# Eight strips of a Strassen-multiplied up-projection opened ahead of the norm, their partial sums kept in DRAM

## The chip, the cores and the metric

One Trainium2 chip, one core. The metric is the device time of one execution in microseconds (us). The engines are named as in the profile: PE is TensorE, DVE is VectorE, ACT is ScalarE, POOL is GpSimd, SP is SyncE, whose queue issues the DMAs. Each engine works through its instructions in order.

## What is computed

A decoder trunk of two layers on 1024 tokens of width 1024, in float32. Layer 0 mixes tokens by a gated linear recurrence (HGRN2, 8 heads), layer 1 by latent attention (MLA, 8 heads). Each mixer is followed by a gated feed-forward network of width 2816 with a causal convolution of three taps, and that is what the change is about:

```python
def _conv_ffn(h, w_up, conv_w, conv_b, w_down):
    S = h.shape[1]
    u = h @ w_up
    u_pad = jnp.pad(u, ((0, 0), (FFN_CONV - 1, 0), (0, 0)))
    y = conv_b.astype(u.dtype)
    for j in range(FFN_CONV):
        y = y + u_pad[:, j:j + S, :] * conv_w[j]
    gate, up = jnp.split(y, 2, axis=-1)
    return (jax.nn.silu(gate) * up) @ w_down

def reference(...):
    ...
    for layer in range(DEPTH):
        h = _rmsnorm(x, norm_mix[layer])
        ...
        x = x + y
        h = _rmsnorm(x, norm_ffn[layer])
        x = x + _conv_ffn(h, ffn_w_up[layer], ffn_conv_w[layer], ffn_conv_b[layer], ffn_w_down[layer])
    return x
```

## The kernel before

**Layout and precision.** The residual x lies with its channels on the 128 partitions, as two tiles `xt[0]` and `xt[1]` of 8 x 512 tokens: x0 holds the first 512 tokens, x1 the last. Every float32 product is made of three matmuls: each operand is split into a high part (a cast, ACT, line 125) and a low part (a subtraction, DVE or POOL, line 128), and high x high, low x high and high x low are summed in PSUM.

**The up-projection** (`up_phase`) runs over 22 strips a layer. Strip j makes 128 gate channels and 128 up channels for all 1024 tokens. It is cut in 2 x 2 blocks (gate or up channels; lower or upper half of the input channels) against 2 x 2 blocks of the normed input (lower or upper half of the channels; x0 or x1), and multiplied in Winograd's form of Strassen's algorithm, which takes seven block products. A product (`product`, line 835) is 12 matmuls of 128 x 512. The operands on the side of the input are b11 and b21, which need x0 alone, and t1, t2, t3, r22 and t4, which need x0 and x1. On the side of the weights, `combos` (line 819) forms s1 to s4 with four adds on DVE and splits all of them; raw weights come into two `wraw` buffers of 512 KB.

The seven products of a strip are, in order: a11 b11 into a bank of PSUM named `ps_mm`, a12 b21 into `ps_wo` (the two *opening* products, which make the gate's result on the first tokens), s2 t2 on top of a11 b11 in `ps_mm`, the previous strip's last product a22 t4 (`tail`), s1 t1 on top, s3 t3 into `ps_up`, and s4 r22 on top. Between them `ps_mm` is read out by ACT copies: line 863 behind the first, 877, 881 and 886 in `middle`. DVE adds the results from `ps_wo` and `ps_up` (line 849). ACT makes the first tap of the convolution (line 842) and DVE the two others (line 845); ACT applies Silu (889), DVE multiplies gate and up (872), and the strip goes out to DRAM as `act_spill` (873), from which `down_phase` fetches it again (930). The strips' results lie where x was: `normalize` writes x to DRAM (`x_spill`, line 238) and scales it in place (line 242).

**The gap.** Ahead of strip 0 stand `first_half` (norm of x0, b11 and b21 split into the tiles hh0 and hl0) and `second_half` (norm of x1, the differences of line 261, and t2, t1, t3, r22, t4 split on DVE, line 128). `up_phase` emits the combos and the opening products of strips 0 and 1 (`start`), then `second_half`, then the rest of strip 0 and 1, and then strip by strip.

**What sets the order.** The code is written in Tile with its scheduler: the program's order gives the priorities, and a planner sets one fixed order of instructions for each engine before the run. So a block that is emitted earlier tends to stand earlier in each queue, mixed with its neighbours.

**The mixers.** In `hgrn` the loop over (head, half) units emits `first_half` when the next unit is the last (`i + 2 == len(units)`), so ahead of the last recurrence `recur`. The output matmuls `wout` (lines 144 to 146) of the last unit follow it. In `mla` each head runs `attend` for four blocks of queries; the maximum of the scores is a reduction (line 682), then a small maximum (685) and the bias of the exponential (687); the residual add is line 275. The token sums of a norm are matmuls with ones (line 164), and line 218 copies the spread scale that line 242 multiplies with.

Of the kernel before, what the change touches and what calls it, by code (L numbers as in the profile page):

```python
# [9 lines left out]
F32 = mybir.dt.float32  # L10
# [5 lines left out]
ALU = mybir.AluOpType  # L16
# [3 lines left out]
P = 128  # L20
# [38 lines left out]
def trunk_kernel(ctx: ExitStack, tc: tile.TileContext, x, pos, par, gout, cst, msk, w_hin, w_hout,  # L59
# [23 lines left out]
    acts = nc.dram_tensor("act_spill", (NFF, P, S), F32).ap()  # L83

# [150 lines left out]
    LO, HI = slice(0, KH), slice(KH, KD)  # L235

# [17 lines left out]
    def second_half(layer, ep):  # L254
# [23 lines left out]
    def hgrn(layer, h):  # L278
        with ExitStack() as st:
# [186 lines left out]
            for i, (hd, hf) in enumerate(units):  # L466
# [11 lines left out]
                if i + 2 == len(units):  # L478
                    h2 = first_half(layer)
# [27 lines left out]
    def mla(h):  # L507
        with ExitStack() as st:
# [247 lines left out]
            for hd in range(HEADS):  # L756
# [13 lines left out]
                o1 = otile()  # L770
                attend(hd, 2, kk, vv, *q1, *o1)
                wout(0, wo, o0)
# [26 lines left out]
    def up_phase(layer, h, wfp, ps_up):  # L799
        with ExitStack() as st:  # L800
# [4 lines left out]
            def combos(j):  # L805
# [7 lines left out]
                t1 = pair("w", wpool, 3)  # L813
                split(g, *t1, lo_eng=dve)
# [10 lines left out]
                def half(t, i):  # L825
                    return [x[:, i * HF:(i + 1) * HF] for x in t]

                return dict(a11=half(t1, 0), a12=half(t1, 1), s2=half(t2, 0), s4=half(t2, 1), s3=half(t3, 0),
                            s1=half(t3, 1), a22=t4)

            def product(p, a, b, first=True):
                for k in range(KH):
                    ks = slice(k * P, (k + 1) * P)
                    for n, (l, r) in enumerate(((0, 0), (0, 1), (1, 0))):
                        pe.matmul(p, lhsT=a[l][:, ks], rhs=b[:, r, k, :], start=first and k == 0 and n == 0,  # L835
                                  stop=k == KH - 1 and n == 2, skip_group_check=not first)
# [14 lines left out]
            L, R = slice(0, HF), slice(HF, S)  # L851
            ts = {}

            def start(j):
                c = combos(j)
                ug, uu = us[2 * (j % 2)], us[2 * (j % 2) + 1]
                c.update(ug=ug, uu=uu, yb=ps_mm(), wb=ps_wo())
                product(c["yb"], c["a11"], b11)
                product(c["wb"], c["a12"], b21)
                return c  # L860

            def opened(c):
                act.copy(out=c["ug"][:, L], in_=c["yb"])
                add(c["ug"][:, L], c["wb"])

            def tail(j, c):
# [8 lines left out]
            def middle(j, c, prev):  # L875
                product(c["yb"], c["s2"], t2, False)
                act.copy(out=c["uu"][:, L], in_=c["yb"])
                if prev is not None:
                    tail(j - 1, prev)
                product(c["yb"], c["s1"], t1, False)  # L880
                act.copy(out=c["uu"][:, R], in_=c["yb"])
                c["zb"] = ps_up()
                product(c["zb"], c["s3"], t3)
                add(c["uu"][:, R], c["zb"])
                product(c["yb"], c["s4"], r22, False)
                act.copy(out=c["ug"][:, R], in_=c["yb"])
                yg = ys[2 * (j % 2)]
                conv(j, c["ug"], yg)
                act.activation(out=yg, in_=yg, func=AF.Silu)
                c["yg"] = yg  # L890
# [7 lines left out]
            prev = c1  # L898
            for j in range(2, NFF):
# [131 lines left out]
```

## Time and profile before

| | before |
|---|---|
| median of 3 runs | 2642.61 us (2641.17 to 2643.84) |
| the profiled execution | 2641.39 us |
| its span in the profile | 2639.7 us |
| its mean granted TensorE clock | 0.971 |
| busy us (share): PE | 2476.8 (94%) |
| DVE | 1772.4 (67%) |
| ACT | 1048.6 (40%) |
| POOL | 503.5 (19%) |

The profile is of one execution. Times in its rows run from the start of the span. The granted clock is TensorE's, as a share of full speed (1.00 is 2.4 GHz, 0.50 is 1.2 GHz). In a row of the timeline, `[18.60 <-ACT bop L125]` says that the engine had stood idle for 18.60 us and that an ACT instruction of line 125 on tile `bop` released it. A group of several instructions is marked `x8`, and its time reaches from the first start to the last end. Layer 0's up-projection runs from about 718 us, layer 1's from about 1980 us.

### The profile page before, as it was taken

The numbers are of one execution on the slowest core, as the hardware profiler recorded it, in microseconds if no ns is written. First come the engines' busy times: TensorE is split into PE (matmuls) and PEld (weight loads), VectorE is DVE, ScalarE is ACT, GpSimd is POOL, SyncE is SP. The second block draws the span as 40 slices with busy tenths as digits, with TensorE's granted clock in tenths as the row PEclk, the third lists the DMA queues.
The fourth block names the chain that finished last, engine by engine and source line by source line (L and its number), as shares of the span: only waits on it lengthen the run. The fifth ranks groups of instructions, "written<-read, shape, count | busy, mean of one in ns | idle before, by whom it ended". The sixth has DMA issues, their size and how long they took to land.

```text
span 2639.7 us, 35284 instructions
## 1 busy us (share of the span) xinstructions
PE 2476.8 (94%) x13732; PEld 2049.1 (78%) x13732; DVE 1772.4 (67%) x3186; ACT 1048.6 (40%) x1729; POOL 503.5 (19%) x489
## 2 busy tenths in 40 slices
PE   7999999998599999999999999989839999999999
PEld 6888888886388888888887777777628888888887
DVE  7456565578767777774445888788787777775333
ACT  5222222223344444533333544444434444544322
POOL 4343333442000000000013434443300000000000
PEclk9999999998699999999999999999969999999999
DMA  3110110210122222264431000000111222226443
GB/s 143 41 41 33 38 36 24 66 57 33 56 88 72 84 84 81 94 224 152 140 116 40 9 17 17 25 17 9 41 56 71 88 74 94 74 75 221 156 170 121
DMA packets 58343, 203.03 MB, mean 77 GB/s; under 512 B 6592, under 2 KB 6976, under 8 KB 57024
## 3 DMA queue, kind: packets, MB, share of 16 engines
q1 hardware_dynamic: 58176, 200.77, 21.5%
q8 instruction: 108, 1.77, 0.3%
q14 instruction: 59, 0.48, 0.1%
HBM read 165.10 MB, written 35.65 MB: 76 GB/s over the span
## 4 chain that ended last, share of the span: by engine, by line
PE 80%; DVE 15%; ACT 2%; issue 1%; DMA 1%; POOL 0%; SPq 0%; DVEq 0%; ACTq 0%; POOLq 0%
PE ps_mm L835 19%; PE ps_up L835 9%; PE ps_up L924 7%; PE ps_mm L144 6%; PE ps_mm L146 6%; PE ps_mm L145 5%; PE ps_mm L924 4%; PE ps_wo L924 4%; PE ps_wo L835 4%; PE ps_misc L924 2%; DVE x L275 2%; PE sc L364 2%; PE ps_wo L144 2%; PE ps_wo L146 1%; PE sp L677 1%; PE ps_wo L145 1%
## 5 line engine op out<-in xcount | busy, mean ns | idle before, releaser
L125 ACT CAST whi<-wraw 128x1024 fp32r<-128x1024 f32 (+1 forms) x312 | 306.6, 991 | 619.7 <-PE ps_misc L924 234.9
L128 DVE TENSOR_TENSOR wlo<-wraw,whi 128x1024 fp32r<-128x1024 f32 (+1 forms) x266 | 298.2, 1134 | 325.6 <-ACT whi L125 325.4
L835 PE MATMUL ps_mm<-bop,whi 128*128 128x512 f32 x1408 | 446.1, 398 | 21.3 <-ACT bop L125 11.2
L835 PEld LDWEIGHTS ps_mm<-bop,whi 128*128 128x128 f32 x1408 | 268.3, 191 | 84.4 <-ACT bop L125 11.7
L845 DVE SCALAR_TENSOR_TENSOR x<-x,prm,x 128x1023 f32<-128x1023 f32 (+1 forms) x176 | 225.1, 1280 | 103.5 <-ACT x L842 102.8
L835 PE MATMUL ps_mm<-bop,wlo 128*128 128x512 f32 x704 | 277.5, 395 | 0.0
L835 PE MATMUL ps_up<-bop,whi 128*128 128x512 f32 x704 | 221.1, 395 | 36.6 <-ACT bop L125 36.6
L835 PEld LDWEIGHTS ps_up<-bop,whi 128*128 128x128 f32 x704 | 132.4, 188 | 67.6 <-ACT bop L125 37.5
L924 PE MATMUL ps_up<-ring,whi 128*128 128x512 f32 x528 | 159.3, 389 | 0.0
L835 PEld LDWEIGHTS ps_mm<-bop,wlo 128*128 128x128 f32 x704 | 134.1, 191 | 30.1
L128 POOL TENSOR_TENSOR wlo<-wraw,whi 128x1024 fp32r<-128x1024 f32 x46 | 112.3, 2444 | 221.6 <-ACT whi L125 221.3
L144 PE MATMUL ps_mm<-vgh,hh 128*128 128x256 f32 x512 | 145.1, 284 | 5.4 <-DVE q L331 5.4
L146 PE MATMUL ps_mm<-vgh,hl 128*128 128x256 f32 x512 | 145.1, 283 | 0.0
L145 PE MATMUL ps_mm<-vgl,hh 128*128 128x256 f32 x512 | 143.7, 281 | 0.0
L835 PE MATMUL ps_up<-bop,wlo 128*128 128x512 f32 x352 | 138.2, 393 | 0.0
L375 DVE TENSOR_TENSOR Q<-Q,tot 128x256 f32<-128x256 f32 x96 | 61.1, 636 | 100.8 <-PE sc L364 78.7
L677 PE MATMUL sp<-kk,qq 128*128 128x256 f32 (+4 forms) x480 | 112.2, 364 | 15.4 <-ACT pp L692 11.9
L819 DVE TENSOR_TENSOR wraw<-wraw 128x512 f32<-128x512 f32 x176 | 122.4, 695 | 1.2
L144 PE MATMUL ps_mm<-hh,whi 128*128 128x512 f32 x288 | 116.4, 404 | 2.5 <-DVE g L351 1.6
L842 ACT ACTIVATE x<-x,prm 128x1024 f32<-128x1024 f32 x88 | 109.4, 1243 | 15.3 <-DVE x L849 13.8
L377 POOL TENSOR_TENSOR K<-K,tot 128x256 f32<-128x256 f32 x96 | 77.2, 805 | 199.3 <-PE sc L364 125.4
L924 PEld LDWEIGHTS ps_up<-ring,whi 128*128 128x128 f32 x528 | 99.1, 188 | 20.5
(302 smaller groups left out, 5790.5 us busy)
## 6 DMA issues: line engine op xcount, KB each, us to landing
wraw<-in_w_up_dram SPq DMA_DIRECT2D x88, 512.0 KB, 3.8
wraw<-in_w_down_dram SPq DMA_DIRECT2D x88, 512.0 KB, 3.5
act_spill<-x SPq DMA_DIRECT2D x44, 512.0 KB, 2.6
araw<-act_spill SPq DMA_DIRECT2D x88, 256.0 KB, 3.6
wraw<-in_w_hin_dram SPq DMA_DIRECT2D x38, 512.0 KB, 3.5
x_spill<-x SPq DMA_DIRECT2D x4, 2048.0 KB, 7.3
x<-x_spill SPq DMA_DIRECT2D x4, 2048.0 KB, 8.1
wraw<-in_w_hout_dram SPq DMA_DIRECT2D x8, 512.0 KB, 3.5
```

The lines of the kernel that those rows point to most:

```text
L125: act.copy(out=hi, in_=src)
L128: lo_eng.tensor_tensor(out=lo, in0=src, in1=hi.bitcast(F32), op=ALU.subtract)
L144: pe.matmul(ps, lhsT=lh, rhs=rh, start=(i == 0), stop=False)
L145: pe.matmul(ps, lhsT=lh, rhs=rl, start=False, stop=False)
L146: pe.matmul(ps, lhsT=ll, rhs=rh, start=False, stop=(i == n - 1))
L377: pool.tensor_tensor(out=Kv[:, :, 0, :], in0=Kv[:, :, 0, :], in1=tv[:, :, 1:2].broadcast_to([P, nb, m]), op=ALU.mult)
L677: pe.matmul(sp[:, 0:n], lhsT=qq[:, a, qs], rhs=kk[:, c, cl], start=(i == 0), stop=last)
L819: dve.tensor_tensor(out=o, in0=p, in1=q, op=op)
L835: pe.matmul(p, lhsT=a[l][:, ks], rhs=b[:, r, k, :], start=first and k == 0 and n == 0, stop=k == KH - 1 and n == 2, skip_group_check=not f ...
L842: act.activation(out=y, in_=u, func=AF.Identity, scale=cw(2, ff), bias=pcol("cb", layer * 44 + ff))
L845: dve.scalar_tensor_tensor(out=y[:, i:S], in0=u[:, 0:S - i], scalar=cw(2 - i, ff), in1=y[:, i:S], op0=ALU.mult, op1=ALU.add)
L924: pe.matmul(acc[d], lhsT=w[l][:, d * P:(d + 1) * P], rhs=a[:, r], start=j == 0 and n == 0, stop=j == NFF - 1 and n == 2)
```

## The change

1. `second_half` is emitted first in `up_phase`. Behind it a new `open_strips` makes the two opening products of the eight strips 1, 3, 5, ..., 15 (`OPENED`). For each it fetches and splits the gate weights, runs a11 b11 into a `ps_mm` bank, copies it out (R), runs a12 b21 on top, and copies the sum out (L), both by ACT. The copies lie in small tiles (one buffer for R, two for L) and are stored to a DRAM tensor `open_spill`, 256 KB each.
2. In its turn, an opened strip fetches R and L from `open_spill` (512 KB) straight into the place of the gate's result, and makes five products. Its reads of `ps_mm` are then DVE adds with R, where a plain strip has ACT copies; the split of the gate weights and the add of the second opening product fall away. `start`, `opened` and `middle` become one function `strip`, and strips 0 and 1 no longer have their combos and opening products ahead of `second_half`.
3. In `hgrn`, `first_half` is emitted behind the last recurrence (`i + 1 == len(units)`), ahead of its `wout`.
4. In the last head of `mla`, the first `wout` is emitted ahead of the third `attend`.
5. t1 and t2 trade tiles with t3 and r22.

```diff
+    OPENED = tuple(range(1, 17, 2))
...
+    def open_strips(layer, h):
+        b11, b21 = h
+        for j in OPENED:
+            a11, a12 = halves(load_w(w_up[layer][j], eng=dve))
+            p = ps_mm()
+            for a, b, to, tag in ((a11, b11, R, "rb0"), (a12, b21, L, "sq")):
+                product(p, a, b, to is R)
+                t = tpool.tile([P, HF], F32, tag=tag, name="part", bufs=2 if tag == "sq" else 1)
+                act.copy(out=t, in_=p)
+                nc.sync.dma_start(out=opening[j][:, to], in_=t)
...
-        t2 = operand(f2, hpool, "hh1")
-        t1 = operand(b11, hpool, "hl1")
+        t2 = operand(f2, ep, "e0")
+        t1 = operand(b11, ep, "e1")
...
-        t3 = operand(b12, ep, "e0")
-        r22 = operand(b22, ep, "e1")
+        t3 = operand(b12, hpool, "hl1")
+        r22 = operand(b22, hpool, "hh1")
...
-                if i + 2 == len(units):
+                if i + 1 == len(units):
                     h2 = first_half(layer)
...
+                if not more:
+                    wout(0, wo, o0)
                 attend(hd, 2, kk, vv, *q1, *o1)
-                wout(0, wo, o0)
+                if more:
+                    wout(0, wo, o0)
...
-                t1 = pair("w", wpool, 3)
-                split(g, *t1, lo_eng=dve)
+                c = {}
+                if not opened:
+                    t1 = pair("w", wpool, 3)
+                    split(g, *t1, lo_eng=dve)
+                    c["a11"], c["a12"] = halves(t1)
...
+            def strip(j, prev):
+                opened = j in OPENED
+                c = combos(j, opened)
...
+                if opened:
+                    nc.sync.dma_start(out=ug, in_=opening[j])
+                else:
+                    product(yb, c["a11"], b11)
+                    act.copy(out=ug[:, L], in_=yb)
+                    wb = ps_wo()
+                    product(wb, c["a12"], b21)
+                    add(ug[:, L], wb)
+
+                def read(dst):
+                    if opened:
+                        dve.tensor_tensor(out=dst, in0=ug[:, R], in1=yb, op=ALU.add)
+                    else:
+                        act.copy(out=dst, in_=yb)
+
+                product(yb, c["s2"], t2, opened)
+                read(uu[:, L])
...
-            c0, c1 = start(0), start(1)
             t1, t2, t3, t4, r22 = second_half(layer, ep)
-            opened(c0)
-            opened(c1)
-            middle(0, c0, None)
-            middle(1, c1, c0)
...
+            open_strips(layer, h)
+            prev = None
+            for j in range(NFF):
+                prev = strip(j, prev)
+            tail(prev)
```

The planner's order shows what moves. Three places of DVE's queue follow; a row has the line, the operation, the tiles out<-in and the shape.

The first place is the end of `second_half` in layer 0. `x_73` and `x_74` are x0's and x1's tiles, `f_...` the difference of which t2 is made, `bop` an operand's low part, `wlo` that of a weight. Before:

```order
L819 TENSOR_TENSOR wraw<-wraw 128x512 x4
L128 TENSOR_TENSOR wlo<-wraw,whi 128x1024
L242 SCALAR_TENSOR_TENSOR x_74<-x_74,prm,rb 128x512 x8
L128 TENSOR_TENSOR wlo<-wraw,whi 128x1024
L261 TENSOR_TENSOR x_73<-x_74,x_73 128x2048
L128 TENSOR_TENSOR bop<-x_74,bop 128x2048
L261 TENSOR_TENSOR f_6986<-x_74,x_73 128x2048
L261 TENSOR_TENSOR x_74<-x_74 128x2048
L128 TENSOR_TENSOR bop<-x_73,bop 128x2048
L261 TENSOR_TENSOR x_73<-x_73,f_6986 128x2048
L128 TENSOR_TENSOR bop<-f_6986,bop 128x2048
L128 TENSOR_TENSOR bop<-x_74,bop 128x2048
```
And with the change:

```order
L129 TENSOR_TENSOR wlo<-wraw,whi 128x1024
L129 TENSOR_TENSOR bop<-x_73,bop 128x2048
L129 TENSOR_TENSOR wlo<-wraw,whi 128x1024
L285 TENSOR_TENSOR x_73<-x_73,f_6886 128x2048
L129 TENSOR_TENSOR bop<-f_6886,bop 128x2048
L129 TENSOR_TENSOR bop<-x_74,bop 128x2048
L129 TENSOR_TENSOR wlo<-wraw,whi 128x512
L129 TENSOR_TENSOR bop<-x_73,bop 128x2048
L870 TENSOR_TENSOR x_73<-x_73,ps_wo 128x512
L849 TENSOR_TENSOR wraw<-wraw 128x512 x4
L129 TENSOR_TENSOR wlo<-wraw,whi 128x1024 x2
L129 TENSOR_TENSOR wlo<-wraw,whi 128x512
```
The four combination adds of strip 0 (line 819, now 849), which stood ahead of x1's scaling, now stand behind the last operand, and so do the low parts made of them; low parts of the openers' weights stand between the operands.

The second place is in strips 5 and 6 of layer 0 (5 is opened), with combination adds and low parts of weights, and the adds from PSUM. Before, in such strips:

```order
L872 TENSOR_TENSOR x_74<-x_74 128x1024
L819 TENSOR_TENSOR wraw<-wraw 128x512
L128 TENSOR_TENSOR wlo<-wraw,whi 128x1024 x2
L849 TENSOR_TENSOR x_73<-x_73,ps_wo 128x512
L845 SCALAR_TENSOR_TENSOR x_74<-x_73,prm,x_74 128x1023
L845 SCALAR_TENSOR_TENSOR x_74<-x_73,prm,x_74 128x1022
L849 TENSOR_TENSOR x_73<-x_73,ps_up 128x512
L128 TENSOR_TENSOR wlo<-wraw,whi 128x1024
L128 TENSOR_TENSOR wlo<-wraw,whi 128x512
```
With the change:

```order
L849 TENSOR_TENSOR wraw<-wraw 128x512 x2
L890 TENSOR_TENSOR x_73<-x_73,ps_mm 128x512
L129 TENSOR_TENSOR wlo<-wraw,whi 128x1024
L870 TENSOR_TENSOR x_73<-x_73,ps_up 128x512
L129 TENSOR_TENSOR wlo<-wraw,whi 128x1024
L890 TENSOR_TENSOR x_73<-x_73,ps_mm 128x512
L866 SCALAR_TENSOR_TENSOR x_74<-x_73,prm,x_74 128x1023
L129 TENSOR_TENSOR wlo<-wraw,whi 128x512
L866 SCALAR_TENSOR_TENSOR x_74<-x_73,prm,x_74 128x1022
```
The new reads of `ps_mm` (line 890) stand just ahead of low parts (129), in the queue that also has the adds (870) and taps (866).

The third place is the end of the attention in layer 1, from the last low part of the probabilities (`tl`) to the bias `nb` of the last block. Before:

```order
L128 TENSOR_TENSOR tl<-ps_wo,th 128x384
L696 RECIPROCAL sm<-sm 128x1
L682 TENSOR_REDUCE mx<-sp 128x1
L819 TENSOR_TENSOR wraw<-wraw 128x512
L212 TENSOR_TENSOR acc<-acc,sq 128x512
L275 TENSOR_TENSOR x_73<-x_73,ps_mm 128x512 x2
L685 TENSOR_TENSOR mx<-mx 128x1
L819 TENSOR_TENSOR wraw<-wraw 128x512
L128 TENSOR_TENSOR ol<-ps_misc,oh 128x256
L687 SCALAR_TENSOR_TENSOR nb<-mx,rq 128x1
```
With the change:

```order
L129 TENSOR_TENSOR tl<-ps_wo,th 128x384
L706 TENSOR_REDUCE mx<-sp 128x1
L299 TENSOR_TENSOR x_73<-x_73,ps_mm 128x512
L709 TENSOR_TENSOR mx<-mx 128x1
L711 SCALAR_TENSOR_TENSOR nb<-mx,rq 128x1
L299 TENSOR_TENSOR x_73<-x_73,ps_mm 128x512
L213 TENSOR_TENSOR acc<-acc,sq 128x512
L299 TENSOR_TENSOR x_73<-x_73,ps_mm 128x512
L719 TENSOR_TENSOR sm<-sm 128x1
L129 TENSOR_TENSOR ol<-ps_misc,oh 128x256
```
The combination adds of strips 0 and 1 (819) no longer stand between the maximum and the bias.

## Rows read from the trace of the kernel before

A row of the windows has the stretch, its length, then the busy time of PE, PEld (weight loads), DVE, ACT and POOL.

**Rows 1.** Page, part 1: busy us, share and instructions of each engine.
```profile
PE 2476.8 (94%) x13732; PEld 2049.1 (78%) x13732; DVE 1772.4 (67%) x3186; ACT 1048.6 (40%) x1729; POOL 503.5 (19%) x489
```
**Rows 2.** Windows, steady up-projection: us, busy us (instructions), PEclk, DMA share, GB/s.
```profile
760.00:1120.00 360.00, 360.00 (x1568) 294.08 (x1567) 272.79 (x302) 174.54 (x207) 0.00 (x0) 1.00 0.24 84
...
2022.00:2382.00 360.00, 360.00 (x1568) 294.05 (x1568) 272.54 (x302) 174.45 (x207) 0.00 (x0) 1.00 0.24 84
```
**Rows 3.** Groups by form, VectorE, 760:1120: count, busy, mean ns, idle, releasers.
```profile
L128 DVE TENSOR_TENSOR wlo<-wraw,whi 128x1024 fp32r<-128x1024 f32 x56 | 67.5, 1223 | 41.5 <-ACT whi L125 41.5
L819 DVE TENSOR_TENSOR wraw<-wraw 128x512 f32<-128x512 f32 x76 | 52.2, 687 | 0.4
L845 DVE SCALAR_TENSOR_TENSOR x<-x,prm,x 128x1023 f32<-128x1023 f32 x37 | 47.4, 1282 | 37.6 <-ACT x L842 37.6
...
L849 DVE TENSOR_TENSOR x<-x,ps_wo 128x512 f32<-128x512 f32 x19 | 13.0, 685 | 5.6 <-PE ps_wo L835 5.6
```
**Rows 4.** Windows of the gap ahead of layer 0's up-projection.
```profile
660.00:680.00 20.00, 13.50 (x48) 8.38 (x47) 13.22 (x30) 9.02 (x19) 3.87 (x3) 0.83 0.11 45
680.00:700.00 20.00, 10.00 (x34) 8.03 (x34) 14.99 (x33) 4.35 (x5) 0.00 (x0) 0.69 0.39 140
700.00:720.00 20.00, 3.87 (x7) 2.40 (x8) 20.00 (x12) 10.09 (x6) 0.00 (x0) 0.50 0.00 0
```
**Rows 5.** Windows of the gap ahead of layer 1's up-projection.
```profile
1940.00:1960.00 20.00, 11.57 (x51) 9.08 (x49) 11.83 (x28) 3.20 (x4) 0.00 (x0) 0.84 0.08 27
1960.00:1980.00 20.00, 1.61 (x3) 0.60 (x3) 20.00 (x15) 8.22 (x6) 0.00 (x0) 0.50 0.00 0
```
**Rows 6.** Timeline of TensorE: start, us, instruction [idle <-releaser]; openings, restarts.
```profile
717.72 0.79 PE L835 MATMUL ps_mm<-bop,whi 128*128 128x512 f32 x1 [2.99 <-DVE bop L128]
...
1935.01 0.79 PE L835 MATMUL ps_mm<-bop,whi 128*128 128x512 f32 x1 [11.18 <-ACT bop L125]
...
1949.31 0.95 PE L164 MATMUL ps_misc<-ones,acc 128*128 128x2 f32 x8
...
1979.98 0.79 PE L835 MATMUL ps_mm<-bop,whi 128*128 128x512 f32 x1 [3.00 <-DVE bop L128]
```
**Rows 7.** Timeline of VectorE, from x1's norm to the restart, layer 0.
```profile
695.73 5.39 DVE L242 SCALAR_TENSOR_TENSOR x<-x,prm,rb 128x512 f32<-128x512 f32 x8 [1.08 <-ACT rb L218]
...
715.38 2.29 DVE L128 TENSOR_TENSOR bop<-f,bop 128x2048 fp32r<-128x2048 f32 x1
717.58 2.29 DVE L128 TENSOR_TENSOR bop<-x,bop 128x2048 fp32r<-128x2048 f32 x1
```
**Rows 8.** Groups by form, ScalarE, 760 to 1120.
```profile
L125 ACT CAST whi<-wraw 128x1024 fp32r<-128x1024 f32 x57 | 58.8, 1050 | 63.4 <-DMA wraw<-in_w_up_dram 42.5 <-DVE wraw L819 14.3 <-PE ps_mm L835 5.6
...
L863 ACT COPY x<-ps_mm 128x512 f32<-128x512 f32 x19 | 11.2, 587 | 68.0 <-PE ps_mm L835 68.0
```
**Rows 9.** Timeline of VectorE at the end of the attention, layer 1.
```profile
1896.29 0.67 DVE L682 TENSOR_REDUCE mx<-sp 128x1 f32<-128x512 f32 x1
1896.88 1.14 DVE L819 TENSOR_TENSOR wraw<-wraw 128x512 f32<-128x512 f32 x1
...
1898.55 1.27 DVE L275 TENSOR_TENSOR x<-x,ps_mm 128x512 f32<-128x512 f32 x2
...
1900.74 0.14 DVE L687 SCALAR_TENSOR_TENSOR nb<-mx,rq 128x1 f32<-128x1 f32 x1
```
**Rows 10.** Page, part 6: DMA issues, KB each, median us to landing.
```profile
wraw<-in_w_up_dram SPq DMA_DIRECT2D x88, 512.0 KB, 3.8
...
act_spill<-x SPq DMA_DIRECT2D x44, 512.0 KB, 2.6
...
x_spill<-x SPq DMA_DIRECT2D x4, 2048.0 KB, 7.3
```
**Rows 11.** Windows of the last recurrence of layer 0.
```profile
600.00:620.00 20.00, 18.75 (x206) 15.79 (x205) 17.26 (x49) 8.68 (x26) 9.96 (x12) 1.00 0.00 1
620.00:640.00 20.00, 14.79 (x150) 11.34 (x150) 18.29 (x59) 6.65 (x19) 6.61 (x8) 0.83 0.25 106
```

More of the change, by code (lines that the diff above doesn't have):

```diff
@@ L83, in trunk_kernel @@
     acts = nc.dram_tensor("act_spill", (NFF, P, S), F32).ap()
+    opening = nc.dram_tensor("open_spill", (NFF, P, S), F32).ap()
     def fetch_w(src):
@@ L235, in trunk_kernel, with halves, product @@
     LO, HI = slice(0, KH), slice(KH, KD)
+    OPENED = tuple(range(1, 17, 2))
+    L, R = slice(0, HF), slice(HF, S)
+    def halves(t):
+        return [[x[:, i * HF:(i + 1) * HF] for x in t] for i in range(2)]
+    def product(p, a, b, first=True):
+        for k in range(KH):
+            ks = slice(k * P, (k + 1) * P)
+            for n, (l, r) in enumerate(((0, 0), (0, 1), (1, 0))):
+                pe.matmul(p, lhsT=a[l][:, ks], rhs=b[:, r, k, :], start=first and k == 0 and n == 0,
+                          stop=k == KH - 1 and n == 2, skip_group_check=not first)
+    def open_strips(layer, h):
[8 more added lines that the diff above has]
+                nc.sync.dma_start(out=opening[j][:, to], in_=t)
     def normalize(hf, layer):
@@ L823, in combos @@
                 split(u, *t3, lo_eng=dve)
[L825 to L836, printed above, removed]
+                (c["s2"], c["s4"]), (c["s3"], c["s1"]) = halves(t2), halves(t3)
+                c["a22"] = t4
+                return c
             def cw(i, ff):
@@ L849, in add, with tail @@
                 dve.tensor_tensor(out=dst, in0=dst, in1=p, op=ALU.add)
[L851 to L855, printed above, removed]
+            def strip(j, prev):
+                opened = j in OPENED
+                c = combos(j, opened)
+                c["j"] = j
                 ug, uu = us[2 * (j % 2)], us[2 * (j % 2) + 1]
-                c.update(ug=ug, uu=uu, yb=ps_mm(), wb=ps_wo())
-                product(c["yb"], c["a11"], b11)
-                product(c["wb"], c["a12"], b21)
-                return c
[L862 to L866, printed above, removed]
+                c["uu"] = uu
+                yb = ps_mm()
+                if opened:
[13 more added lines that the diff above has]
+                read(uu[:, L])
+                if prev is not None:
+                    tail(prev)
+                product(yb, c["s1"], t1, False)
+                read(uu[:, R])
+                c["zb"] = ps_up()
+                product(c["zb"], c["s3"], t3)
+                add(uu[:, R], c["zb"])
+                product(yb, c["s4"], r22, False)
+                read(ug[:, R])
+                yg = ys[2 * (j % 2)]
+                conv(j, ug, yg)
+                act.activation(out=yg, in_=yg, func=AF.Silu)
+                c["yg"] = yg
+                return c
+            def tail(c):
+                j = c["j"]
                 product(c["zb"], c["a22"], t4, False)
@@ L873, in tail @@
                 nc.sync.dma_start(out=acts[j], in_=yg)
[L875 to L890, printed above, removed]
-            c0, c1 = start(0), start(1)
-            t1, t2, t3, t4, r22 = second_half(layer, ep)
-            opened(c0)
-            opened(c1)
-            middle(0, c0, None)
-            middle(1, c1, c0)
-            prev = c1
-            for j in range(2, NFF):
-                c = start(j)
-                opened(c)
-                middle(j, c, prev)
-                prev = c
-            tail(NFF - 1, prev)
+            t1, t2, t3, t4, r22 = second_half(layer, ep)
+            open_strips(layer, h)
+            prev = None
+            for j in range(NFF):
+                prev = strip(j, prev)
+            tail(prev)
     def down_phase(layer, wfp, ps_up):
```

2 lines of the change are left out of this document (1 added, 1 removed).

## The prediction

> **What bounds the kernel now.** I read the busy shares first. TensorE is busy 94% of the span, VectorE 67%, ScalarE 40% [rows 1]; so time can be won where TensorE stands still, or by taking work off it. The stretches come next. In the steady part of the up-projection TensorE is busy all of 360 us, at a granted clock of 1.00, in either layer [rows 2]. In it 76 combination adds run, four a strip [rows 3], so 19 strips go by. One strip is seven products, so a product costs 360/(19 x 7) = **2.71 us**, or 226 ns for each of its 12 matmuls. VectorE has 272.8 us of work there, 14.36 a strip against TensorE's 18.95.
>
> Before that stretch TensorE starves. From 660 to 720 us it is busy 13.5, 10.0 and 3.9 of 20, the clock goes down to 0.50, and VectorE is full at the end [rows 4]; from 1940 to 1980 it is busy 11.6 and 1.6 [rows 5]. The timelines of the two engines say why: TensorE restarts at 717.72 and 1979.98 on an operand's low part [rows 6]. The first is VectorE's row at 715.38, the last but one in a row of whole-tile operations of 2.29 us (2.20 from start to start) that begins with the scaling of x1 at 695.73 [rows 7]. That chain is x1's norm and the differences; TensorE can only fill the time, not shorten it.
>
> **A, products moved into the gap.** Before, four opening products (of strips 0 and 1) lie in front of the restart in each layer. Now 18 do: two for each of eight opened strips, and strip 0's two. So 14 products a layer leave the part in which TensorE is never idle: 14 x 2.71 = 37.9, for both layers **-75.9 us**. Is there room? In layer 0 TensorE is idle for 60 - 27.4 = 32.6 us from 660 to 720 [rows 4], and the restart comes 10.8 us later (B): 43 us for 38. In layer 1 it is idle 8.4 + 18.4 = 26.8 us [rows 5], waits 11.2 us before its first opening matmul at 1935.01 [rows 6], and restarts 7.3 us later (B): 45 us, of which some at the front goes while weights and x0's operands come. I take the whole 75.9 us; the lower end is 62, when 2.5 products a layer don't fit.
>
> The Trainium skill, "TensorE: Matmul & The Clock Gate", section "Wait — 56ns, not 53.3ns?", gives 215.7 ns from start to start for 512 columns on a warm engine, which would make A 72.5 us by an estimate from that page; the 226 ns of this trace differ from it and stand.
>
> **B, the restart itself.** Before, strip 0's four combination adds were done ahead of x1's norm. Now VectorE has them behind all differences and operands. Between the low part of t2 (the f row of 715.38), which released TensorE, and the low part of strip 0's s2 now stand an operand 2.20 [rows 7], a 512-wide low part 0.69 (as an add of that width), an operand 2.20, an add from PSUM 0.69, four combination adds 4 x 0.687 = 2.75 [rows 3], and then s2 itself: ScalarE's cast 1.05 [rows 8] and the low part 1.22. That is 10.8 us in layer 0. The chain up to t2 I leave where it is there: it loses the low parts that stood in it, gets as many new ones, and has the last recurrence free of x0's norm ahead; ends -5 and +5, two steps of 2.2 us and a bit, since the token sums of x1 now stand behind opening matmuls on TensorE. In layer 1 two more low parts, 1024 wide and 1.2 each, stand in the chain, and the add runs beside the cast: 12.5 us. Against that t2 comes earlier. At the end of the attention 4.45 us pass from the last head's maximum at 1896.29 to the bias made from it at 1900.74 [rows 9]; of what stands there the maximum (0.59 to the next start), one residual add of the two (0.6) and the small maximum (0.1) remain, so 3.2 us go. And x1's token sums at 1949.31 stand behind four opening products on TensorE [rows 6], now behind two: 5.4 us. Low parts of openers on VectorE take 1.2 + 2.2 back. That makes 5.2 us earlier, net 7.3. Together **+18 us**, ends 8 and 28.
>
> **C, opened strips lean on VectorE.** An opened strip has five products, 13.55 us on TensorE, but on VectorE its reads of PSUM become three adds: 14.36 - 1.22 (low part of g) - 0.685 (add of the second product) + 3 x 0.685 = 14.51 us [rows 3]. With the plain strip that follows, a pair has 28.87 us of VectorE against 12 x 2.71 = 32.5 of TensorE. Were VectorE never to wait, it would be covered. But it waits now 41.5/19 = 2.2 us a strip for ScalarE's cast and 37.6/19 = 2.0 for ScalarE's first tap of the convolution [rows 3]. If both stay, the pair takes 28.87 + 8.4 = 37.3, 4.7 us over TensorE. The new adds stand, by the order of VectorE's instructions, right ahead of low parts that wait for casts; if the three fill 2.1 us of such waits, 35.2 us are left, 2.7 over TensorE. The other waits have work of the next strip behind them that can begin early in some places and not in others, so I take **1.5 us a pair**, about half way between nothing and 2.7. Eight pairs in two layers: 16 x 1.5 = **+24 us**; ends 0 and 16 x 4.7 = 75.
>
> **What costs nothing.** The stores (256 KB, at most the 2.6 us of a 512 KB store) and fetches (at most 3.8 us) [rows 10] have a strip pair of 32.5 us, with the DMA engines at 0.24 [rows 2]; an opening copy and its store's landing, 0.59 [rows 8] + 2.6 = 3.2 us, fit into the 5.4 us of an opened strip's two products, which the single buffer of R needs. If this cover goes, TensorE waits for PSUM in the gap (third rival). The fetches of gate weights again, 16 times 512 KB, are on the same queue and have the same cover. ScalarE loses 64 copies and gains 32; at 40% of the span [rows 1] it isn't the bound. The exchange of operand tiles and the earlier output matmuls of the last head move nothing on the chain but what B counts.
>
> **The sum.** -75.9 + 18 + 24 = -33.9 on the profiled execution's own 2641.4 us, so 2607.5; the median of the runs lies 1.2 us above that execution, so about **2608 us**. C at 0.5 or 2.5 us a pair moves it by 16 either way, and B by 8 more, most of the way to its ends: the forecast's own range is 2584 to 2632.
>
> **The rivals.**
> 1. *VectorE keeps up.* C is 0 and B near 8: 2641.4 - 75.9 + 8 + 0 + 1.2 = 2575, and up to 2584. For it: 28.87 us of work under 32.5 [rows 2, 3]. Against it: waits of 4.2 us a strip that no row shows shrinking. Chance 0.18.
> 2. *VectorE becomes the bound in the opened strips*, with both waits whole: 37.3 us a pair, 2642.6 - 75.9 + 18 + 75 = **2660**, slower. It decides from 57.9/16 = 3.6 us lost a pair, a pair above 36.1 us. For it: the new adds read what TensorE has just finished and stand before the casts' low parts in the same in-order queue. Against it: they fill the time in which VectorE now waits. Chance 0.11.
> 3. *The gap fills by half.* The opening copies wait for the single buffer and its store, and that store stands on the one queue with spills of x (2 MB, 7.3 us [rows 10]) that wait for x; seven products a layer run behind the restart after all, 38 us back: 2608 + 38 = 2646, no difference. For it: those spills have stood at the head of the queue. Against it: weights of the openers go out ahead of them. Chance 0.07.
> 4. *The clock falls in the up-projection.* At 600 to 620 us TensorE is busy 18.75 of 20 with the clock at 1.00; in the next 20 it is busy 14.79 and has 0.83 [rows 11]. If opened strips leave gaps in which it falls so, the 8 x 32.5 + 19 = 279 us a layer become 336, 57 more each: 2608 + 114 = 2722. Against it: pairs that are 1.5 us over leave TensorE busy for over 95% of the time, more than either row. Chance 0.02. The Trainium skill, "TensorE: Matmul & The Clock Gate", section "A second HAM failure mode: psum-queue depth-cycling", tells of a clock that goes up and down when small idle times stand between groups of matmuls. The up-projection of this trace has no such case.
>
> **How the numbers follow.** A measurement of this kernel tells about 0.2%, 5.3 us, from no change. The forecast has 0.62; rival 1, 0.18, is also faster: 0.80. Rival 3 is mostly within 5.3 us: 0.05, with 0.02 slower. Slower: 0.11 + 0.02 + 0.02 = 0.15. The range of 8 in 10 reaches from rival 1 to rival 3, 2576 to 2648, and leaves out the slow cases and the lower part of the first.
>
> **What would show it.** A: TensorE busy nearly all of 660 to 720 and 1940 to 1980, with 36 products in front of the restarts. B: restarts at about 728.5 and 1987, released by a low part behind four combination adds. C: pairs of 34 us in the stretch of strips 1 to 16, TensorE waiting there for VectorE 1.5 us a pair, and none behind strip 16. Wrong would be it if the pairs take over 36 us, if TensorE is idle over 10 us in a gap, or if the granted clock in the opened stretch is under 0.95.

## The result and the profile after

| | before | after |
|---|---|---|
| median | 2642.73 us (2641.17 to 2643.84, 4 runs) | **2607.93 us** (2607.36 to 2608.78, 4 runs) |
| ratio after / before | | 0.9869, 95% interval 0.9852 to 0.9886 |
| the profiled execution, its span | 2641.39, 2639.7 us | 2608.18, 2606.4 us |
| mean granted clock | 0.971 | 0.982 |

The kernel is 1.3% faster, and the time is the predicted one: the prediction's sum for the profiled execution was 2607.5 us, and it took 2608.2. Two of the three terms were not as predicted: one was 10 us too small and another 9 us too large, for a wrong reason. The rows below show the first part of this, the experiments the second.

The page's first part answers to [rows 1]. TensorE's work is the same; VectorE has 23 us more, ScalarE 22 us less:

```profile
PE 2474.9 (95%) x13732; PEld 2043.3 (78%) x13732; DVE 1795.3 (69%) x3218; ACT 1026.1 (39%) x1697; POOL 504.7 (19%) x489
```

The windows of the two gaps, with the columns of [rows 4, 5]:

```profile
660.00:680.00 20.00, 17.73 (x68) 12.98 (x68) 11.62 (x19) 6.94 (x9) 1.22 (x1) 0.87 0.22 75
680.00:700.00 20.00, 17.24 (x71) 13.42 (x72) 10.38 (x26) 8.08 (x13) 2.65 (x3) 0.91 0.46 180
700.00:720.00 20.00, 19.73 (x87) 15.84 (x86) 20.00 (x17) 14.06 (x16) 0.00 (x0) 1.00 0.45 166
720.00:740.00 20.00, 13.77 (x53) 10.68 (x53) 14.70 (x12) 5.95 (x7) 0.00 (x0) 0.83 0.31 104
...
1940.00:1960.00 20.00, 19.96 (x89) 16.14 (x88) 18.34 (x15) 12.73 (x15) 0.00 (x0) 1.00 0.47 163
1960.00:1980.00 20.00, 18.78 (x81) 14.52 (x80) 17.52 (x15) 10.24 (x12) 0.00 (x0) 1.00 0.40 148
```

Where TensorE was busy 13.5, 10.0 and 3.9 of 20 us it is now busy 17.7, 17.2 and 19.7, and the clock that had gone down to 0.50 stands at 1.00 in the same stretch. Layer 1's gap is full. A new hole is at 720 to 740.

The restarts and ends of the up-projections, in TensorE's timeline of the kernel after (columns as in [rows 6]):

```profile
733.57 1.22 PE L247 MATMUL ps_mm<-bop,whi 128*128 128x512 f32 x2 [6.23 <-ACT whi L126]
...
1128.26 0.39 PE L247 MATMUL ps_up<-bop,wlo 128*128 128x512 f32 x1
...
1921.45 1.22 PE L247 MATMUL ps_mm<-bop,whi 128*128 128x512 f32 x2 [10.41 <-ACT bop L126]
...
1979.15 0.50 PE L247 MATMUL ps_mm<-bop,wlo 128*128 128x512 f32 x1 [0.95 <-DVE wlo L129]
...
2368.66 0.39 PE L247 MATMUL ps_up<-bop,wlo 128*128 128x512 f32 x1
```

And the last products in the kernel before:

```profile
1140.86 0.39 PE L835 MATMUL ps_up<-bop,wlo 128*128 128x512 f32 x1
...
2403.44 0.39 PE L835 MATMUL ps_up<-bop,wlo 128*128 128x512 f32 x1
```

A row gives the start of an instruction and its length, so the last products end at 1128.65 and 2369.05 us, before at 1141.25 and 2403.83. Layer 0's up-projection ends 12.6 us earlier and layer 1's 34.8; the rest of the kernel gives 1.5 back (span: -33.3). With these rows the terms can be measured:

- **A.** Two products a strip of seven moved for eight strips; 168 matmuls a layer should stand in front of the restart that stood behind it; 167 and 169 more are recorded there. One takes 0.230 us (from the strips' stores, below), so 38.7 us a layer, 77.3 together.
- **B.** Layer 0 restarts at 733.57 in place of 717.72, 15.9 us later. In layer 1 the restart is 1979.15 - 1128.65 = 850.5 us behind the end of layer 0's products, before 1979.98 - 1141.25 = 838.7: 11.8 later. Together 27.6.
- **C.** From restart to end, before 423.5 and 423.9 us, after 395.1 and 389.9. With 38.7 us of work less, 10.2 and 4.7 us were lost: 14.9 together.
- -77.3 + 27.6 + 14.9 = -34.8, and +1.5 behind the last product make the -33.3 of the span.

VectorE's timeline says why layer 0's restart is so late. After:

```profile
692.93 0.16 DVE L176 TENSOR_SCALAR st_v<-ps_misc 128x4 f32<-128x4 f32 x1 [6.73 <-PE ps_misc L165]
...
700.99 5.39 DVE L266 SCALAR_TENSOR_TENSOR x<-x,prm,rb 128x512 f32<-128x512 f32 x8
...
721.77 2.29 DVE L129 TENSOR_TENSOR bop<-f,bop 128x2048 fp32r<-128x2048 f32 x1
...
729.58 2.87 DVE L849 TENSOR_TENSOR wraw<-wraw 128x512 f32<-128x512 f32 x4
...
733.55 2.36 DVE L129 TENSOR_TENSOR wlo<-wraw,whi 128x1024 fp32r<-128x1024 f32 x2 [1.11 <-ACT whi L126]
```

The same step before, where x1's token sums come:

```profile
683.72 0.16 DVE L175 TENSOR_SCALAR st_v<-ps_misc 128x4 f32<-128x4 f32 x1 [2.02 <-PE ps_misc L164]
```

The token sums come 9.2 us later (692.93 in place of 683.72), and VectorE waits 6.73 us for them. TensorE's rows show what they stand behind. After:

```profile
685.23 0.82 PE L247 MATMUL ps_mm<-bop,whi 128*128 128x512 f32 x2 [2.68 <-ACT part L258]
...
691.95 0.95 PE L165 MATMUL ps_misc<-ones,acc 128*128 128x2 f32 x8
...
698.79 0.62 PE L197 MATMUL ps_misc<-dg,ones_r 128*128 128x512 f32 x2
```

And before:

```profile
681.84 1.84 PE L164 MATMUL ps_misc<-ones,acc 128*128 128x2 f32 x8 [3.06 <-DVE acc L213]
...
694.67 0.40 PE L196 MATMUL ps_misc<-dg,ones_r 128*128 128x512 f32 x1
```

The squares of x1 are added up at 686.2 us (before 681.7), since the last output matmuls, from which x1 is made, stand behind opening products. Then the ones matmul stands 5.8 us behind more of them, where it began at once before. The pause of 2.68 us ahead of these has its cause in the change too: the opening product there waits for an opening copy, which stands behind squares of x1 in ScalarE's queue. A part comes back further on: the second matmul that spreads the scale stood 5.9 us behind opening products before (its operand was made at 688.8), and now it stands 1.9 us behind them (696.9). So x1's scaling begins 5.3 us later than in [rows 7], and t2's low part comes 6.4 us later. From the end of that low part to s2 it is 9.5 us: more low parts, four adds, ScalarE's cast, and the start on the high part.

In layer 1 the low part that releases s2 stands in VectorE's queue behind an add from `ps_wo`, and that add waits for TensorE's opening products:

```profile
1977.27 0.69 DVE L870 TENSOR_TENSOR x<-x,ps_wo 128x512 f32<-128x512 f32 x1 [2.35 <-PE ps_wo L247]
```

The steady pace can be read from the stores of strips 8, 10 and 12, issued by SyncE, after:

```profile
899.98 0.33 SPq L919 DMA_DIRECT2D act_spill<-x  x1
...
934.07 0.33 SPq L919 DMA_DIRECT2D act_spill<-x  x1
...
968.15 0.33 SPq L919 DMA_DIRECT2D act_spill<-x  x1
```

and of strips 6 and 14 before:

```profile
858.01 0.33 SPq L873 DMA_DIRECT2D act_spill<-x  x1
...
1012.69 0.33 SPq L873 DMA_DIRECT2D act_spill<-x  x1
```

Before, eight strips took 154.68 us: 19.34 a strip, 2.76 a product, 0.230 a matmul. After, a pair takes 34.09 us where its 144 matmuls need 33.1: 1 us lost a pair. TensorE's row in each of these pairs is

```profile
952.60 0.73 PE L247 MATMUL ps_mm<-bop,whi 128*128 128x512 f32 x2 [0.68 <-ACT x L892]
```

a wait for a ScalarE copy, which itself began when the product before it was done:

```profile
951.96 0.59 ACT L892 COPY x<-ps_mm 128x512 f32<-128x512 f32 x1 [3.50 <-PE ps_mm L247]
```

VectorE does not appear in it. VectorE's own waits, for casts (line 129) and for ScalarE's tap (line 866), are in the 16 strips from 760 to 1040 us

```profile
L129 DVE TENSOR_TENSOR wlo<-wraw,whi 128x1024 fp32r<-128x1024 f32 x41 | 49.0, 1221 | 7.4 <-ACT whi L126 7.4
L866 DVE SCALAR_TENSOR_TENSOR x<-x,prm,x 128x1023 f32<-128x1023 f32 x32 | 41.0, 1280 | 11.2 <-ACT x L863 11.2
```

and 3.0 us for casts 512 wide: 1.35 us a strip, where [rows 3] have 4.2. In the first pairs there is more: 1.62 us of waiting for a cast at 848.35, and in the 20 us around it the clock was granted at 0.91 only:

```profile
840.00:860.00 20.00, 18.16 (x72) 14.02 (x71) 14.64 (x17) 8.78 (x10) 0.00 (x0) 0.91 0.31 105
860.00:1000.00 140.00, 137.30 (x594) 110.82 (x593) 120.78 (x137) 64.00 (x71) 0.00 (x0) 1.00 0.30 106
```

The transfers took about what [rows 10] let expect, and no wait is for a fetch from `open_spill`. Four of ScalarE's copies wait for a store of a part, 11.3 us together and 3.9 at most; TensorE waits 3.2 us for copies, of which 2.68 are the pause above:

```profile
open_spill<-part SPq DMA_DIRECT2D x32, 256.0 KB, 2.3
x<-open_spill SPq DMA_DIRECT2D x16, 512.0 KB, 3.2
```

### The profile page after: what moved, and what is told of

The parts are those of the page before. It is cut to its first block, busy times and chain, and to the rows that moved or that the text cites. A ratio compares the mean times of both kernels' runs of the same rounds, so it can differ in the third digit from the quotient of the medians.

```text
span 2606.4 us, 35442 instructions
## 1 busy us (share of the span) xinstructions
PE 2474.9 (95%) x13732; PEld 2043.3 (78%) x13732; DVE 1795.3 (69%) x3218; ACT 1026.1 (39%) x1697; POOL 504.7 (19%) x489
## 4 chain that ended last, share of the span: by engine, by line
PE 77%; DVE 16%; ACT 3%; issue 2%; DMA 1%; POOL 0%; ACTq 0%; DVEq 0%; SPq 0%; POOLq 0%
PE ps_mm L247 18%; PE ps_up L247 8%; PE ps_up L946 7%; PE ps_mm L145 6%; PE ps_mm L147 6%; PE ps_mm L146 6%; PE ps_mm L946 5%; PE ps_wo L946 4%; PE ps_wo L247 3%; PE sc L388 2%; PE ps_misc L946 2%; DVE x L299 2%; PE sp L701 2%; PE ps_wo L145 1%; DMA wraw<-in_w_up_dram 1%
## 5 line engine op out<-in xcount | busy, mean ns | idle before, releaser
L247 PE MATMUL ps_mm<-bop,whi 128*128 128x512 f32 x1536 | 485.3, 398 | 40.2 <-ACT bop L126 15.8
L247 PEld LDWEIGHTS ps_mm<-bop,whi 128*128 128x128 f32 x1536 | 290.3, 191 | 115.2 <-ACT bop L126 16.3
L247 PE MATMUL ps_mm<-bop,wlo 128*128 128x512 f32 x768 | 299.7, 395 | 0.9 <-DVE wlo L129 0.9
L247 PEld LDWEIGHTS ps_mm<-bop,wlo 128*128 128x128 f32 x768 | 146.2, 190 | 33.6 <-DVE wlo L129 1.4
L247 PEld LDWEIGHTS ps_up<-bop,whi 128*128 128x128 f32 x704 | 132.0, 188 | 32.5 <-ACT whi L126 2.0
L701 PE MATMUL sp<-kk,qq 128*128 128x384 f32 (+4 forms) x480 | 112.1, 363 | 16.6 <-ACT pp L716 13.5
```

The source lines that it names most:

```text
L701: pe.matmul(sp[:, 0:n], lhsT=qq[:, a, qs], rhs=kk[:, c, cl], start=(i == 0), stop=last)
```

## Experiments

Times are medians; the kernel before, run beside each group on the same chip, took 2641.9 (e1 to e4), 2643.6 (e5 to e8), 2644.1 (e9 to e11) and 2646.0 us (e12).

### e1, e2: no opened strip, and four

```diff
-    OPENED = tuple(range(1, 17, 2))
+    OPENED = ()                        # e1
+    OPENED = tuple(range(1, 9, 2))     # e2
```

> The change with no opened strip; the other edits stay. My theory (the gain is the moved products): 32 opening products of 2.76 us go back behind the restart, +88; the waits in opened strips go, some -16; without opening products ahead of x1's token sums the restarts come about 4 us earlier in each layer, -8. So 2608 + 64 = 2672 us (2655 to 2685), slower than before the change. Rival, the other edits (norm of x0 behind the last recurrence, the order of the attention's end) carry the gain: 2608 to 2620 us.

> Four opened strips (1, 3, 5, 7) for eight. My theory: 16 products of 2.76 us go back, +44; half the waits in opened strips go, -8; a little less stands ahead of the restarts, -4: 2640 us (2630 to 2648). Rival, four strips already fill what can be filled: about 2608 us or less. Rival, the gain is of other edits: 2608 to 2620 us.

Measured: e1 **2635.97 us** (ratio to before 0.9974, 0.9961 to 0.9986), e2 **2629.92 us** (0.9945, 0.9923 to 0.9968). The opened strips carry 28 of the 34 us, the other edits 6. e2 came out at the lower edge of its range. But e1 was expected at 2672. Its restarts show the error:

```profile
717.22 0.80 PE L247 MATMUL ps_mm<-bop,whi 128*128 128x512 f32 x1 [2.99 <-DVE bop L129]
...
1975.55 0.80 PE L247 MATMUL ps_mm<-bop,whi 128*128 128x512 f32 x1 [2.99 <-DVE bop L129]
```

Layer 0's is where it was before (717.72), layer 1's is 4.4 us earlier than before (1979.98), and some 50 matmuls of the up-projection are recorded ahead of each, as before. Though strips 0 and 1 are written behind `second_half` there, the planner puts their combinations and opening products into the gap by itself. So the late restart (B) is no price of the new order of the code: it comes with the opening products, whose weights, low parts and matmuls take the places on VectorE and TensorE that strip 0's had. With four strips, 122 and 120 matmuls stand in front (72 and 70 more), and TensorE is still idle 19.0 and 17.4 us at the end of the gaps: they did not fill it. Half the strips gave only a fifth of the opened strips' gain (6 of 28 us), though the 72 and 70 matmuls are 33 us: against e1 the restarts came 6.4 and 5.2 us later already, counted as for B, and in the pairs TensorE waits as in the kernel after.

### e3: the opened strips in a row

```diff
-    OPENED = tuple(range(1, 17, 2))
+    OPENED = tuple(range(1, 9))
```

> The eight opened strips are 1 to 8, in a row, in place of every other one; the products moved are the same. Theory of the prediction (VectorE with its waits sets the pace of an opened strip, and a plain strip beside it gives it slack): an opened strip needs 14.5 us and a part of 4.2 us of waits on VectorE against 13.8 on TensorE, so eight in a row take 15.7 to 18.7 each, 15 to 39 us a layer more than TensorE's own time; against the 5 to 10 us lost now that makes 2625 to 2670 us. Rival (VectorE keeps up; what is lost is one ScalarE copy between two products of a plain strip, 0.9 us a pair): 2600 to 2612 us.

Measured: **2632.56 us** (0.9956, 0.9940 to 0.9972), 25 us slower than the change with the same products moved. TensorE's waits between 740 and 1060 us in this kernel (us in total, times, longest):

```profile
PE ps_mm L247 <- DVE x L890: 14.0, 9, 2.6
PE ps_mm L247 <- ACT x L892: 0.7, 1, 0.7
```

and in the kernel after:

```profile
PE ps_mm L247 <- ACT x L892: 4.6, 7, 0.7
PE ps_mm L247 <- ACT whi L126: 2.1, 2, 1.6
PE ps_up L247 <- ACT whi L126: 0.2, 1, 0.2
```

Here VectorE does hold TensorE up, as the second rival had it: each opened strip waits some 1 to 2.6 us for the add that reads `ps_mm` (line 890). Beside a plain strip it doesn't. Of the 25 us, 20.5 lie between the restarts and the last products (406.1 and 399.4 us, after 395.1 and 389.9). The waits are more than the change's by 8 us in layer 0; besides, the granted clock is 0.91 from 780 to 820 us, where it is 1.00 in the kernel after.

### e4, e8: the norm of x0, moved alone and moved back

```diff
-                if i + 2 == len(units):    # e4, in the kernel before
+                if i + 1 == len(units):
```

```diff
-                if i + 1 == len(units):    # e8, in the changed kernel
+                if i + 2 == len(units):
```

> The kernel before with one edit of the change: the norm of x0 behind the last recurrence. My theory: the gap's length is set by the chain of x1's norm, which this hardly moves; the last recurrence ends some us earlier and x0's operands come later: 2635 to 2645 us. Rival, this edit carries a good part of the gain: under 2630 us.

> The change without its move of x0's norm: it stands ahead of the last recurrence, as before. My theory: with the norm ahead, VectorE is held in the last recurrence and x1's chain begins some 3 us later, but the opening products may begin earlier: 2606 to 2614 us. Rival, the opened strips need this move, since x0's norm among the last recurrence's work would delay the opening products or x1's sums by much: over 2618 us.

Measured: e4 **2638.53 us** (0.9983, 0.9972 to 0.9994), e8 **2611.54 us** (0.9882, 0.9862 to 0.9901). Moved alone the edit gives 3.4 us, and undoing it costs 3.6, which its interval can't tell from nothing. It is a small part of the gain, and the opened strips don't need it. What the rest of the 6 us of the other edits comes from was not tested alone.

### e5: no two products of one bank in a row

The order of a strip's products becomes s2, s3, s1, a22, s4, so that each read of a bank has another product beside it:

```diff
                 product(yb, c["s2"], t2, opened)
                 read(uu[:, L])
-                if prev is not None:
-                    tail(prev)
+                zb = ps_up()
+                product(zb, c["s3"], t3)
+                if opened:
+                    dve.tensor_tensor(out=uu[:, R], in0=ug[:, R], in1=zb, op=ALU.add)
+                else:
+                    act.copy(out=uu[:, R], in_=zb)
                 product(yb, c["s1"], t1, False)
-                read(uu[:, R])
-                c["zb"] = ps_up()
-                product(c["zb"], c["s3"], t3)
-                add(uu[:, R], c["zb"])
+                add(uu[:, R], yb)
+                product(zb, c["a22"], t4, False)
                 product(yb, c["s4"], r22, False)
                 read(ug[:, R])
...
+                add(uu[:, L], zb)
...
```

> The change with the products of a strip in the order s2, s3, s1, a22, s4, so that two products into the same bank of PSUM never follow each other: the s3 product is read out ahead of s1 (a copy, or an add with R), s1 is added from its bank, and a22 of the same strip stands between s1 and s4. The numbers of products, copies and adds stay. My theory now (what a pair loses is one wait for a ScalarE copy between s1 and s4 of the plain strip, 0.68 us in the trace and 0.9 with the slow start behind it): 16 pairs x 0.9 = 14 us less, 2594 us (2588 to 2600). Rival, the theory of the prediction (the pace of a pair is set by VectorE's waits for casts and taps): these stay, 2604 to 2612 us.

Measured: **2590.57 us** (0.9800, 0.9784 to 0.9816), 17 us less than the change. TensorE's waits from 700 to 1110 us are now only

```profile
PE ps_mm L247 <- ACT whi L126: 6.2, 1, 6.2
PE ps_mm L247 <- ACT part L258: 0.3, 1, 0.3
```

the late restart and one copy; layer 1's steady part has two short waits, of 0.84 and 0.50 us. VectorE has the same number of instructions (3218) and the same work (1797 us, 1795 in the change), though its own waits for casts and taps are shorter here too (0.5 us a strip from 760 to 1040). Together with the row of 952.60 this puts what a pair lost on the place of one copy: in the change the planner put s4 of the plain strip right behind s1, in the same bank, with ScalarE's copy between.

### e6, e7: strip 0 opened and its combinations ahead of the gap

```diff
-    OPENED = tuple(range(1, 17, 2))
+    OPENED = tuple(range(0, 17, 2))
...
-            def strip(j, prev):
+            def strip(j, prev, c=None):
                 opened = j in OPENED
-                c = combos(j, opened)
+                c = c or combos(j, opened)
...
+            c0 = combos(0, True)
             t1, t2, t3, t4, r22 = second_half(layer, ep)
             open_strips(layer, h)
...
-                prev = strip(j, prev)
+                prev = strip(j, prev, None if j else c0)
```

e7 has this on top of e5.

> Nine opened strips 0, 2, ..., 16 in place of 1, 3, ..., 15, and strip 0's combinations written ahead of x1's norm; strip 0 needs no opening product at its turn, so 18 products stand in the gap as now. My theory (layer 0's restart is late because strip 0's four adds, cast and low part stand behind the last operand, TensorE idle for 6.2 us there; in layer 1 TensorE is full of opening products and idle for 1 us): 7 us less, 2601 us (2597 to 2605). Rival, the restart is held by the opening products and x1's chain alone: 2606 to 2611 us.

> The edits of the two runs named e5_alternate and e6_even together. If both theories hold and the two losses are apart in time: 2608 - 14 - 7 = 2587 us (2580 to 2594). If only the order within strips holds: 2594; if only the restart: 2601.

Measured: e6 **2625.28 us** (0.9934, 0.9914 to 0.9953), e7 **2608.79 us** (0.9871, 0.9856 to 0.9886): 17 and 18 us slower than the same without the edit. My expectation was wrong. SyncE's queue in e6, layer 0:

```profile
579.46 2.72 SPq L88 DMA_DIRECT2D wraw<-in_w_up_dram  x2
626.59 0.33 SPq L262 DMA_DIRECT2D x_spill<-x  x1
677.61 0.33 SPq L262 DMA_DIRECT2D x_spill<-x  x1
678.99 0.33 SPq L88 DMA_DIRECT2D wraw<-in_w_up_dram  x1
```

and TensorE's first opening product there:

```profile
687.26 1.22 PE L247 MATMUL ps_mm<-bop,whi 128*128 128x512 f32 x2 [2.98 <-ACT whi L126]
```

In the kernel after, SyncE's one row ahead of the spills is

```profile
579.03 14.16 SPq L88 DMA_DIRECT2D wraw<-in_w_up_dram  x5
```

The change issues five weight fetches ahead of both spills of x, and TensorE opens at 659.55. In e6 strip 0's two raw weights go out first and fill the two `wraw` buffers until VectorE makes their low parts (677.74 to 680.10); the first opener's weights are issued behind x1's spill, at 678.99, and TensorE opens at 687.26, 28 us later. What the restart wins, and more, is lost at the front of the gap: layer 0's last product ends 8.3 us later than in the change. This is not the third rival itself, which held the opening copies up by their buffer and store, but its neighbour: e6 takes away the reason that stood against that rival, that the openers' weights go out ahead of the spills.

### e9, e10: nine and ten opened strips on e5

```diff
-    OPENED = tuple(range(1, 17, 2))
+    OPENED = tuple(range(1, 19, 2))    # e9
+    OPENED = tuple(range(1, 21, 2))    # e10
```

> The kernel of e5_alternate with nine opened strips (1, 3, ..., 17). In layer 0 TensorE is idle for 6.2 us ahead of strip 0's s2 product, so two more opening products (5.5 us) stand there for nothing; in layer 1 TensorE is full from the first opening product on, so there they cost what they save. My theory: 2590.6 - 5.5 = 2585 us (2582 to 2589). Rival, more openers push x1's chain and the restart further back (low parts on VectorE, copies on ScalarE): 2590 to 2596 us.

> The same with ten opened strips (1, 3, ..., 19). The idle time in layer 0 is used up with nine, so nothing more is won: 2583 to 2589 us by my theory. Rival, each opened strip beyond costs some us in its restart: over 2590 us. Rival, opened strips are cheaper than plain ones even without a gap: under 2582 us.

Measured: e9 **2584.55 us** (0.9770, 0.9754 to 0.9787), e10 **2580.26 us** (0.9756, 0.9741 to 0.9770). In e9 the 6.2 us of idle time ahead of layer 0's s2 are 0.95:

```profile
737.65 0.50 PE L247 MATMUL ps_mm<-bop,wlo 128*128 128x512 f32 x1 [0.95 <-DVE wlo L129]
```

as expected. The tenth strip was expected to give nothing and the median is 4 us lower, below my range, though the two intervals overlap. It meets the range of the rival that opened strips are cheaper than plain ones (under 2582), but this isn't shown: a pair takes 33.0 us by its stores, the time of its 144 matmuls. Between the two profiled executions 2.1 of 4.4 us lie ahead of layer 0's first opening product (660.17 and 658.06), which the edit doesn't touch, and e9 has four short waits in the two up-projections that e10 lacks (0.95, 0.50, 0.67 and 1.30 us). So what the tenth strip is worth stays open. In e10 TensorE has no wait from 700 to 1110 us but 1.7 us for copies of parts:

```profile
PE ps_mm L247 <- ACT part L258: 1.7, 2, 1.5
```

### e11, e12: the attention's order undone

```diff
-                if not more:
-                    wout(0, wo, o0)
                 attend(hd, 2, kk, vv, *q1, *o1)
-                if more:
-                    wout(0, wo, o0)
+                wout(0, wo, o0)
```

e11 is the change with this edit, e12 is e10 with it.

> The change without its edit of the attention: the last head's first output matmuls stand behind the third block of queries, as before. The run without opened strips was 3.6 us shorter in layer 1 than before, which I put down to this edit: 2611 to 2612 us. Rival, what shortened it are the combinations that left the end of the attention, not the output matmuls: 2607 to 2609 us.

> The kernel of e10_ten with the edit of the attention undone. That edit undone alone gave 2606.0 us against 2607.9 for the change. Theory, the edit costs some 2 us: 2578 us (2576 to 2580). Rival, the difference was chance of the two runs or of the planner's order: 2580 to 2583 us.

Measured: e11 **2605.97 us** (0.9853, 0.9833 to 0.9872), e12 **2582.00 us** (2577.92 to 2586.25; 0.9764, 0.9744 to 0.9783). e11 lies under both ranges, e12 in the rival's. Both intervals hold the value of the kernel that has the attention's edit (0.9869 and 0.9756). This edit is worth nothing that can be told here.

## Why the prediction was right, and where it wasn't

**What bounds.** Right: the gap's length was set by x1's norm and operands, and could be filled, not shortened. e1, with no opened strip, has the same gap: TensorE idle 17.7 and 18.0 us ahead of its restarts, released by an operand's low part as before.

**A, 75.9 us: measured 77.3.** The step that was a little off is the count of strips in the 360 us. 76 combination adds belong to 19 strips, but not the same 19 whose matmuls run there; the 1568 matmuls of [rows 2] are 18.67 strips of 84. So a product is 2.76 us, not 2.71. The room was about as estimated: layer 0's gap holds nine strips (e9), layer 1's was full with eight (18.8 to 20.0 of 20 us busy).

**B, +18 us: measured +27.6, at the end of its bounds.** The part behind t2 came as worked out: 9.5 us in layer 0, which is the 10.8 without the low part (1.2), as TensorE began on the high part. Wrong was the sentence that left "the chain up to t2" where it was. It came 6.4 us later in layer 0, because the output matmuls that complete x1 and the ones matmul for its token sums stand in TensorE's queue behind opening products. I had this as the +5 end and not as the value. In layer 1 the restart wasn't set by this chain any more: TensorE has opening products from 1921 to 1977 us, with pauses of 1.1 and 0.3 us, VectorE's add waits for the last of them, and TensorE then waits 0.95 us for the low part. So the sum by which t2 comes 5.2 us earlier had nothing to act on; counted from the end of layer 0's products, t2's low part came 2.6 us earlier (833.8 us behind them, before 836.4). The 4.5 us by which this restart is later than forecast (11.8 and 7.3) are products that did not fit, some 1.6 of them. A had kept this case for its lower end; it is booked under B here.

**C, +24 us: measured +14.9, and for another reason.** The forecast of a steady pair, 34.0 us, was met by 34.09. But it was 32.5 + 1.5 with 1.5 from VectorE's waits, and it is 33.1 + 1.0 with 1.0 lost at a ScalarE copy between two products of one bank (0.68 of it is the wait itself). The premise that failed is that no row shows VectorE's waits shrinking: they went from 4.2 us a strip to 1.35, so that the 28.9 us of work that C counts for a pair and 2.7 us of waits fit under TensorE's 33.1. e5 takes that copy out of TensorE's way and the loss is gone with VectorE's work unchanged. The mechanism that I had priced exists: with the opened strips in a row (e3) TensorE waits for VectorE's adds at each. The plain strip between two opened ones is what keeps it off.

**What costs nothing.** The opening copies were to be covered. Four of them wait for their buffer's store, and one holds TensorE up for 2.68 us; it is booked under B.

**The sum** was right because B's error (+9.6) and C's (-9.1) cancel. The sign and the size of the gain come from A, which was sound; that the sum is met within a microsecond is luck.

**The signs.** The pairs of 34 us came, the granted clock stayed over 0.95 but for 20 us, and TensorE was busy 54.7 of 60 us from 660 to 720 and 38.7 of 40 from 1940 to 1980. The restarts named, 728.5 and 1987, did not come (733.57 and 1979.15), and the second could not: it left out the time that layer 0 saves ahead of layer 1. By one sign the forecast was wrong: TensorE is idle 11.5 us from 660 us to layer 0's restart, more than the 10 named, and 6.2 of them are the late restart.

**The rivals.** VectorE keeps up (first): true for the steady pairs, but the time of that rival needed B near 8 as well. VectorE becomes the bound (second): not here, shown by e3 for another choice of strips. The gap fills by half (third): not here; e6 shows a near relation, one queue and two buffers. Clock (fourth): 1.00 in the 20 us stretches from 740 to 900 us but for one at 0.91 behind a wait of 1.6 us; in e3, with longer waits, 0.91 over 40 us.

## What to carry to other kernels

When independent work is put into an engine's gap, price what then stands behind it: the small matmul that the critical chain needs next now queues behind the filler, and buffers and queue places that the filler needs early must not be given to anything else. Accumulating products into one bank with a read between each needs another bank's product in between; look at the planner's order for two in a row, since the program's order doesn't promise it (e5: 17 us here). And take a time per unit from equal marks of successive units, such as their stores, not from a count of instructions between arbitrary borders.

The best version that ran is e10, the change with that order and ten opened strips: 2580.26 us, ratio 0.9756 (0.9741 to 0.9770) to before.

## What had not been expected of the hardware

Behind a wait of 1.62 us in an otherwise nearly full stretch, TensorE's matmuls ran at half pace for a while: from 850.13 to 851.83 the steps are 0.42 us for one matmul where 0.23 is usual:

```profile
850.13 0.63 PE L247 MATMUL ps_mm<-bop,wlo 128*128 128x512 f32 x1
850.55 1.05 PE L247 MATMUL ps_mm<-bop,whi 128*128 128x512 f32 x2
851.41 0.63 PE L247 MATMUL ps_mm<-bop,wlo 128*128 128x512 f32 x1
```

The waits of 0.68 us, one in each pair, had nothing of this behind them: from 860 to 1000 us the granted clock is 1.00. Nor had one of 1.15 us in layer 1, at 2056.01: from 2040 to 2080 us it is 1.00.
